# A hybrid RWKV-7 decoder step on one core: engine clocks with measured overheads, steps emitted by VectorE's backlog, and a transposed block made by a transposition

## The chip, the cores and the metric

The kernel runs on one core of a Trainium2 chip. The metric is device microseconds from launch to end, the median of several executions of the compiled program. Five engines work side by side, each through its own queue in order: TensorE (PE, with its weight loads shown as PEld), VectorE (DVE), ScalarE (ACT), GpSimd (POOL) and SyncE (SP), which here only starts transfers.

## The reference

One layer of a decoder for 1024 prompt tokens and 8 sequences of 8 tokens (1088 columns in all), with D_MODEL 1024. Cut to what matters:

```python
h = rms_norm(x) * (1 + sc) + sh
P = h @ w_in                       # 1024 x 4352: RWKV columns, pooling columns, gates
# RWKV-7 branch, 8 heads of 64, after token shift:
sa = einsum(S, -kk_t)
S  = S * w_t + sa * (kk_t * a_t) + v_t * k_t        # one 64x64 state per head and token
y  = einsum(S, r_t)                                  # then group norm, bonus, gate g
# pooling branch: causal means over windows 2, 4, 8, 16 minus the token, a 128x128 map per group
merged = sigmoid(gate_A) * (A @ w_br_rwkv) + sigmoid(gate_B) * (B @ w_br_pool)
x = x + gt * (merged @ w_out)
x = x + gt2 * (square(relu(h2 @ w_ff1)) @ w_ff2)     # h2: a second modulated norm
```

All is float32. The outputs are both y and the new shift, pooling and RWKV states.

## The kernel before, in words

Features lie on the partitions, tokens along the free dimension. A float32 product is made of three products in a rounded format: each weight tile of 128 x 512 is loaded (`wraw`), rounded by ScalarE (`whi`), and its remainder is taken by VectorE or GpSimd (`wlo`); activations are stored likewise in pairs (`hx`). A product then is high x high, high x low, low x high. These products are the tiles `mm` in the profile.

The kernel has two phases. Phase 2, from about 790 us on, holds the output projection and the feed-forward layer. Phase 1, up to there, holds the input projection and the RWKV and pooling branches, and only phase 1 is touched by the change.

In phase 1 the PE's order is written out by a planner, `Pace.run`. It has one background, `stream`, the products of the input projection (34 blocks of 128 output columns, each 72 products, in the order of a list of jobs) followed by those of the pooling output; and four foregrounds, generators that emit small steps between the background's products: `heads` (four pairs of heads, f = 0 to 3, one after another), `chains` (the 16 chunks of 64 tokens of a pair, in sequence), `pools` and `or_rows`. A foreground step yields what it waits for. `Need` is a wait until the step's operands and PSUM banks are forecast to be ready. The forecast comes from `Clocks`, which keeps for every other engine a list of busy stretches, puts each emitted instruction into it at a guessed duration (`place`), and notes when its output will be there. So the planner's time `pace.t` is a guess, and PE itself runs the products in the order that results. If the real operand is later than the guess, PE waits and everything behind it waits too. The order on VectorE, ScalarE and GpSimd is set by the tile framework's own scheduler from the order of emission.

A pair of heads goes through `front` (decay, keys, and their norms, almost all on VectorE over 512 and 576 columns), `scores` with `unit` (64 x 64 score blocks by PE), `inverse` (16 x 16 triangular blocks inverted row by row on VectorE: 15 steps of one product and one reduction), `level` (the 32 x 32 and 64 x 64 blocks joined by PE in small products), `affine`, and then the chain. `bonus` and `post` (group norm and gate of the pair before) run beside `inverse` and `level`; for the last pair `post(3)` runs after its chain. `post(3)` takes its three column pieces one by one: a mean product and a variance product with the block of ones (`kct`), root, reciprocal, affine map, bonus, gate, then the pair `hx` that is the last operand of phase 2's first products.

A job of the background can be held: the job of the second gate block after each pooling group g has `hold = ("op", g)`, so the background gives nothing until `pools` has emitted group g's products (`w<-px,plw`). While it is held, foreground steps alone are emitted.

In `level` the products stand on the 32 x 32 blocks of all chunks: `n16` by `xd` (64 products, `w<-hv,hv`), then the block `nd` by `zd` (64, `w<-iv,hv`) and the transposed one, `zd` by `nd`, for half of the blocks (32, `w<-hv,iv`), which is then copied by VectorE to `x32`; then `ao` by `x32` and `pt` by `z` (32 each). Each of them takes two records in the profile. `inverse` spaces its 15 steps by a fixed time:

```python
            yield 200 + 4 * t * t
```

Of the kernel before, what the change touches and what calls it, by code (L numbers as in the profile page):

```python
# [78 lines left out]
class Clocks:  # L79


    TABLE = {AF.Sqrt: 1, AF.Exp: 2, AF.Tanh: 2}

    def __init__(self, pace):
        self.pace, self.on = pace, False
# [34 lines left out]
    def free(self, key, bufs, k=1):  # L120

        ring = self.slots.get(key, [])
        return max([self.last(ring[j - bufs]) for j in range(k) if len(ring) >= bufs - j] or [0.0])

    def place(self, eng, t, ns):

        b = self.busy[eng]
        k = len(b)
        while k and b[k - 1][0] >= t + ns:
            k -= 1  # L130
        for i in range(max(k - 12, 0), len(b) + 1):
            lo = max(t, b[i - 1][1] if i else 0.0)
            if i == len(b) or b[i][0] >= lo + ns:
                b.insert(i, (lo, lo + ns))
                return lo
        return t

    def op(self, eng, name, a, kw):
        aps = [x for x in list(a) + list(kw.values()) if hasattr(x, "tensor")]
        out, ins = aps[0], aps[1:]  # L140
        n = math.prod(out.shape[1:])
        if "dma" in name:
            t = max([self.pace.t - 4000, self.touch(out, False)] + [self.touch(x, True) for x in ins])
            t += 2000 + out.shape[0] * n * 4 / 220 if out.shape[0] <= P else 4000
        else:
            m = max([n] + [math.prod(x.shape[1:]) for x in ins])
            if eng == "scalar":
                ns = 160 + 0.9 * n
                tb = self.TABLE.get(next((x for x in a[2:3]), None), 0)
                if tb and tb != self.table:  # L150
                    ns, self.table = ns + 1300, tb
            elif eng == "gpsimd":
                ns = 250 + (0.5 if "memset" in name else 2.2) * m
            elif name == "reciprocal":
                ns = 60 + 6.65 * n
            elif name == "transpose":
                ns = 2.05 * n
            elif "scan" in name:
                ns = 150 + 2.1 * n
            elif "reduce" in name:  # L160
                ns = 90 + 1.25 * m
            else:
                ns = 150 + (0.8 if name == "tensor_scalar" else 1.05 if n > 100 else 1.6) * n
            ns += 60
            t = max([self.pace.t - 4000, self.touch(out, False)] + [self.touch(x, True) for x in ins])
            t = self.place(eng, t, ns) + ns + 120
        for x in ins:
            self.note(x, t, True)
        self.note(out, t, False)
# [41 lines left out]
class Need:  # L211
# [4 lines left out]

    def at(self):
        return max([self.k.clocks.ready(*self.aps)] + [self.k.clocks.free(b, self.k.pb[b], self.banks.count(b)) for b in set(self.banks)])

    def __call__(self):  # L220
        return self.at() <= self.k.pace.t
# [82 lines left out]
class K:  # L304
# [37 lines left out]
    def product(self, out, *ins):  # L342
        if self.clocks.on:
            for x in ins:
                self.clocks.note(x, self.pace.t, True)
            self.clocks.note(out, self.pace.t + 180, False)

    def need(self, *aps, banks=("w",), wait=500):
        return Need(self, aps, banks, wait)
# [415 lines left out]
    def front(self, f):  # L765

        nc, io = self.nc, self.io
# [8 lines left out]
        k, kk = self.wt(), self.wt()  # L776
# [31 lines left out]
        for c0, n in FH:  # L808
            s, cs = slice(c0, c0 + n), slice(c0 // 64, (c0 + n) // 64)
            t, a, x = t1[:, s], tha[:, s], k[:, s]  # L810
            nc.vector.tensor_scalar(t, t, 1.0, None, op0=ALU.add)
            nc.vector.tensor_tensor_scan(t, self.kscan[:, :n], t, 0.0, ALU.mult, ALU.add)
            m = min(n, NPR - c0)
            nc.scalar.activation(ev[:, c0 // 64:(c0 + m) // 64, 1:65], cut(t1[:, c0:c0 + m]), AF.Exp, scale=-HC)
            if m < n:
                nc.scalar.activation(es[:, :, 1:9], cut8(t1[:, NPR:NT]), AF.Exp, scale=-HC)
            nc.scalar.activation(t, t, AF.Exp, scale=HC)

            nc.vector.scalar_tensor_tensor(kk[:, s], x, self.par("k_k", f), kk[:, s], op0=ALU.mult, op1=ALU.mult)
            g = bk[:, cs, 0, :]  # L820
            nc.vector.tensor_scalar(g, cut(a), self.hp[:, 8 + f:9 + f], self.hp[:, 12 + f:13 + f], op0=ALU.mult, op1=ALU.add)
            nc.vector.tensor_tensor(cut(x), cut(x), g, op=ALU.mult)
            nc.vector.scalar_tensor_tensor(a, a, 1.0, kk[:, s], op0=ALU.add, op1=ALU.mult)
            for h, hs in enumerate(HB):
                nc.vector.tensor_tensor(bk[hs, cs, h, :], cut(x[hs]), cut(t[hs]), op=ALU.mult)
                nc.vector.scalar_tensor_tensor(bk[hs, cs, 1 - h, :], cut(a[hs]), 0.5, cut(t[hs]), op0=ALU.mult, op1=ALU.mult)
            if c0 == 0:
                self.cur = dict(bk=bk, end=end, kk=kk, r=r, ev=ev, es=es, z=self.z, qs={})
# [3 lines left out]
        yield X(8 + f)  # L832
        nc.vector.scalar_tensor_tensor(k, r, self.par("r_k", f), k, op0=ALU.mult, op1=ALU.mult)
        q = [self.row(self.p1, "wt", 5, F32R) for _ in range(2)]
        self.halves(k, *q)
# [118 lines left out]
    def inverse(self, d):  # L954
# [15 lines left out]
        for t in range(1, 16):  # L970
            pr = prod[:, :2 * t * t].rearrange("p (b j i) -> p b j i", b=2, i=t)
            nc.vector.tensor_tensor(pr, at[:, :, t, 0:t].unsqueeze(2).to_broadcast([P, 2, t, t]),
                                    tt[:, :, 0:t, 0:t].rearrange("p b i j -> p b j i"), op=ALU.mult)
            nc.vector.tensor_reduce(tt[:, :, t, 0:t], pr, axis=AX.X, op=ALU.add)
            yield 200 + 4 * t * t
        ex = self.iv()
        nc.scalar.activation(quad(ex)[:, :, :, 0, :], tt, AF.Copy, scale=half[0])
        nc.vector.tensor_scalar(quad(ex)[:, :, :, 1, :], tt, half[1], None, op0=ALU.mult)
# [11 lines left out]
    def level(self, d):  # L990
# [1126 lines left out]
```

## Time and profile before

| | |
|---|---|
| median of 3 runs | 1656.93 us (1653.83 to 1658.22) |
| the profiled execution's own time | 1658.37 us |
| its span in the profile | 1656.5 us |
| PE busy | 1585.9 us, 96% of the span |
| VectorE busy | 1093.8 us, 66% |
| ScalarE busy | 677.1 us, 41% |
| mean granted TensorE clock | 0.977 |

The profiled execution lasts 1.9 us longer than its span (launch and end) and is 1.4 us above the median of the runs. Rows of the profile name an instruction as output<-inputs by the program's names; for a product the moving operand stands first, the stationary one second. "Idle before" is the time that the engine stood still just before the instruction, with what ended it. The granted clock is the share of full speed that TensorE was given.

### The profile page before, as it was taken

To read this page: it belongs to the slowest core of one execution; us is meant where nothing else is said; L and a number is where in the kernel's file an instruction comes from. 1 tells how busy PE (TensorE), PEld (TensorE's weight loads), DVE (VectorE), ACT (ScalarE), POOL (GpSimd) and SP (SyncE) were. 2 spreads that over 40 slices of the span, in tenths; PEclk is the share of its full clock that TensorE was granted. 3 is DMA by queue.
4 is the path that set the end of the run, shared out by engine and by line. 5 is a ranking of instruction groups with operands and counts; after the bars stand their busy time and mean duration, and the time that the engine had idled before them with its cause. 6 is when DMAs were issued, how large, how long until landed. Compare 5 with 4: busy or idle time off the path is not lost.

```text
span 1656.5 us, 35576 instructions
## 1 busy us (share of the span) xinstructions
PE 1585.9 (96%) x14619; PEld 1485.1 (90%) x14619; DVE 1093.8 (66%) x1916; ACT 677.1 (41%) x1299; POOL 135.4 (8%) x200
## 2 busy tenths in 40 slices
PE   4999999989899889999999999999999999999997
PEld 2899888878788779988989999999999999999997
DVE  5576638583948474746543578999866887666775
ACT  4454344444334453443222455222333443434551
POOL 0110001000100010000430130000000042000000
PEclk9999999997999899999999999999999999999999
DMA  9232513323223313474687446566434997655663
GB/s 346 86 108 87 196 47 111 99 90 112 70 104 129 103 55 114 175 276 147 223 326 238 159 160 223 187 222 228 158 141 146 374 359 263 201 198 164 210 203 121
DMA packets 121859, 288.31 MB, mean 174 GB/s; under 512 B 21120, under 2 KB 26752, under 8 KB 121696
## 3 DMA queue, kind: packets, MB, share of 16 engines
q1 hardware_dynamic: 113312, 264.65, 46.2%
q10 hardware_dynamic: 8240, 20.95, 3.8%
q8 instruction: 115, 1.88, 0.5%
q14 instruction: 48, 0.39, 0.1%
q0 software_dynamic: 144, 0.44, 0.1%
HBM read 208.70 MB, written 77.28 MB: 173 GB/s over the span
## 4 chain that ended last, share of the span: by engine, by line
PE 47%; DMA 3%; DVE 3%; issue 1%; POOL 0%; ACT 0%; SPq 0%; DVEq 0%; ACTq 0%; POOLq 0%
PE mm L340 31%; PE wc L340 10%; PE w L340 5%; DMA hid<-in_w_ff 1%; DVE hx L184 1%; DMA hid<-in_w_ada_mlp 1%; DMA mg<-in_w_ff 1%; DVE wlo L184 0%; DMA t<-d_t 0%; DVE mg L184 0%; DMA d_t<-hx 0%; POOL t L184 0%; DVE t L184 0%; DVE sw L184 0%; PE wc L359 0%
## 5 line engine op out<-in xcount | busy, mean ns | idle before, releaser
L340 PE MATMUL mm<-hx,whi 128*128 128x362 f32 (+2 forms) x2944 | 695.2, 324 | 2.9 <-ACT px L184 1.8
L340 PEld LDWEIGHTS mm<-hx,whi 128*128 128x128 f32 x2944 | 502.3, 192 | 31.7 <-issue 16.3
L340 PE MATMUL mm<-hx,wlo 128*128 128x362 f32 (+2 forms) x1472 | 466.1, 317 | 2.2 <-DVE wlo L184 1.8
L340 PEld LDWEIGHTS mm<-hx,wlo 128*128 128x128 f32 x1472 | 282.1, 192 | 2.8 <-DVE wlo L184 2.1
L340 PE MATMUL mm<-mg,whi 128*128 128x272 f32 (+2 forms) x1312 | 249.6, 289 | 0.1
L340 PEld LDWEIGHTS mm<-mg,whi 128*128 128x128 f32 x1312 | 205.6, 189 | 4.5 <-issue 3.4
L340 PE MATMUL mm<-mg,wlo 128*128 128x272 f32 (+2 forms) x656 | 188.5, 287 | 0.0
L340 PE MATMUL wc<-hx,whi 128*128 128x272 f32 x896 | 170.5, 287 | 0.0
L340 PEld LDWEIGHTS wc<-hx,whi 128*128 128x128 f32 x896 | 140.3, 188 | 0.0
L184 ACT ACTIVATE whi<-hid 128x512 fp32r<-128x512 f32 x128 | 80.4, 630 | 140.5 <-PE mm L340 57.3
L340 PE MATMUL wc<-hx,wlo 128*128 128x272 f32 x448 | 128.9, 288 | 1.1 <-DVE wlo L184 1.1
L340 PEld LDWEIGHTS mm<-mg,wlo 128*128 128x128 f32 x656 | 123.5, 188 | 0.0
L184 DVE TENSOR_TENSOR wlo<-hid,whi 128x512 fp32r<-128x512 f32 x128 | 88.0, 688 | 47.1 <-ACT whi L184 46.4
L184 DVE TENSOR_TENSOR wlo<-wraw,whi 128x512 fp32r<-128x512 f32 x84 | 60.9, 726 | 78.4 <-ACT whi L184 78.2
L184 ACT ACTIVATE whi<-wraw 128x512 fp32r<-128x512 f32 x100 | 62.8, 628 | 104.2 <-PE mm L340 65.2
L340 PE MATMUL w<-hx,whi 128*128 128x272 f32 (+1 forms) x480 | 97.8, 298 | 0.0
L340 PEld LDWEIGHTS wc<-hx,wlo 128*128 128x128 f32 x448 | 84.2, 188 | 1.4 <-DVE wlo L184 1.3
L184 POOL TENSOR_TENSOR hx<-hx,rs 128x64 f32<-128x64 f32 x24 | 38.2, 1592 | 565.1 <-DMA mg<-in_w_ff 376.6
L340 PEld LDWEIGHTS w<-hx,whi 128*128 128x128 f32 x480 | 77.8, 190 | 0.0
L340 PEld LDWEIGHTS mm<-mg,hx 128*128 128x128 f32 x576 | 72.9, 188 | 5.0 <-issue 5.0
L340 PE MATMUL mm<-mg,hx 128*128 128x272 f32 (+2 forms) x576 | 75.5, 290 | 0.0
L184 DVE RECIPROCAL wt<-wt 128x182 f32<-128x182 f32 (+3 forms) x52 | 57.6, 1160 | 22.0 <-ACT wt L184 22.0
(270 smaller groups left out, 2391.9 us busy)
## 6 DMA issues: line engine op xcount, KB each, us to landing
t<-d_t SPq DMA_DIRECT2D x56, 544.0 KB, 5.0
hid<-in_w_ff SPq DMA_DIRECT2D x110, 256.0 KB, 3.9
d_t<-hx SPq DMA_DIRECT2D x102, 272.0 KB, 2.2
hid<-in_w_ff SPq DMA_DIRECT2D x42, 512.0 KB, 3.9
wraw<-in_w_in SPq DMA_DIRECT2D x68, 256.0 KB, 2.9
mg<-in_w_ff SPq DMA_DIRECT2D x58, 256.0 KB, 5.4
hid<-in_w_ada_mlp SPq DMA_DIRECT2D x24, 512.0 KB, 5.2
d_th<-px SPq DMA_DIRECT2D x22, 544.0 KB, 3.0
```

The costliest lines, as they stand in the source:

```text
L184: return f(*a, **kw)
L340: return self.nc.tensor.matmul(out, lhsT, rhs, **kw)
```

## The change

Three things, all in phase 1.

The forecast: an instruction of VectorE now occupies its engine for its duration less 80 ns, one of ScalarE for its duration less 95 ns, one of GpSimd for 60 ns less (before: 60 ns more for each), and its output is forecast 60 ns after the duration (before: 180 ns after it).

The emission: a new wait, `Room`, holds a step until the forecast backlog of VectorE is at most 1000 ns (in `front`, twelve times per pair) or 500 ns (in `inverse`, in place of the fixed spacing).

The level: the 32 transposed products and the two copies go; VectorE transposes the 32 x 32 blocks of the product `ps` straight from PSUM into `x32`, and one PSUM bank less is asked for.

```diff
+    OVER = {"vector": 80, "scalar": 95}
...
+    def backlog(self, eng):
+        return max([b[1] for b in self.busy[eng][-12:]] or [0.0])
...
-            ns += 60
             t = max([self.pace.t - 4000, self.touch(out, False)] + [self.touch(x, True) for x in ins])
-            t = self.place(eng, t, ns) + ns + 120
+            t = self.place(eng, t, ns - self.OVER.get(eng, 60)) + ns + 60
...
+class Room:
+    wait = 0
+    def at(self):
+        return self.k.clocks.backlog(self.eng) - self.ns
+    def __call__(self):
+        return self.at() <= self.k.pace.t
...
+    def room(self, ns=1000, eng="vector"):
+        return Room(self, eng, ns)
...
         for c0, n in FH:
+            yield self.room()
             nc.vector.tensor_scalar(t, t, 1.0, None, op0=ALU.add)
...
-            yield 200 + 4 * t * t
+            yield self.room(500)
...
-        yield self.need(nd, zd, banks=("w", "w"))
-        ps, px = self.ps("w"), self.ps("w")
+        yield self.need(nd, zd)
+        ps = self.ps("w")
...
-        for c in range(16):
-            for g in G[::2]:
-                self.mm(at(px, g, c), zd[g, c, :], nd[g, c, :], **tp(g))
         x32 = cut32(self.hv())
-        for g in G[::2]:
-            nc.vector.tensor_copy(x32[g], cut32(px)[g])
+        nc.vector.transpose(x32, cut32(ps))
```

Three places show how the order moves. The first is on PE, pair f = 1, where the background is held on pooling group 1 (`px` and `plw`: that group's products; `bones` with `wt`: sums of `post(0)`; `sw`: its gate; `iv`, `hv`, `ao`, `z`: `level`). Before, these rows stand in one piece, with no background product among them:

```order
L340 MATMUL w_4015<-px_3665,plw_3396 128x364
L340 MATMUL w_4019<-wt_3696,bones 128x364
L340 MATMUL w_4019<-wt_3697,bones 128x364
L340 MATMUL w_4027<-wt_3696,bones 128x362
L340 MATMUL w_4027<-wt_3697,bones 128x362
L340 MATMUL w_4035<-wt_3696,bones 128x362
L340 MATMUL w_4035<-wt_3697,bones 128x362
L340 MATMUL w_4049<-px_3665,plw_3396 128x362
L340 MATMUL w_4053<-wt_4046,sw_4043 128x364
L340 MATMUL w_4056<-iv_3796,hv_3979 32x32 x64
L340 MATMUL w_4057<-hv_3979,iv_3796 32x32 x32
L340 MATMUL w_4161<-hv_4154,ao_3009 32x32 x32
```

Now the group's first two pieces stand among background products (`mm`), 45 of them after the group's own columns are done:

```order
L358 MATMUL mm_3860<-hx_213,whi_3830 128x362
L358 MATMUL mm_3860<-hx_214,whi_3830 128x362
L358 MATMUL mm_3860<-hx_213,wlo_3831 128x362
L358 MATMUL w_3924<-px_3729,plw_3394 128x364
L358 MATMUL w_3928<-px_3729,plw_3394 128x362
L358 MATMUL mm_3858<-hx_215,whi_3830 128x364
L358 MATMUL mm_3858<-hx_216,whi_3830 128x364
```

The third piece and the level's first products follow 18 products later, the level's next 12 later, and the sums of `post(0)` stand far ahead, before the inverse. No background product waits for the hold any more.

The second place is VectorE around the level of pair f = 0 (`iv`, `hv`: the inverse's blocks; `d`, `ds`: token shift of the projection; `am`: a modulation row). Before:

```order
L184 STREAM_TRANSPOSE hv_1890<-iv_1886 128x16x32
L184 STREAM_TRANSPOSE iv_1889<-iv_1886 128x16x32 x2
L184 TENSOR_TENSOR wlo_1936<-wraw_1933,whi_1935 128x512
L184 SCALAR_TENSOR_TENSOR d_1945<-px_1807,part,d_1945 128x1024
L184 SCALAR_TENSOR_TENSOR ds_1946<-px_1807,part,d_1945 128x64
L184 TENSOR_TENSOR hv_2046<-w_1981,kct 128x512
L184 COPY hv_2163<-w_2066 32x512 x2
L184 TENSOR_TENSOR am<-wc_2170,part 128x72
```

After:

```order
L187 STREAM_TRANSPOSE hv_1871<-iv_1867 128x16x32
L187 STREAM_TRANSPOSE iv_1870<-iv_1867 128x16x32 x2
L187 TENSOR_TENSOR wlo_1894<-wraw_1891,whi_1893 128x512
L187 TENSOR_TENSOR hv_1974<-w_1909,kct 128x512
L187 STREAM_TRANSPOSE hv_2049<-w_1984 128x512
L187 TENSOR_TENSOR wlo_2164<-wraw_2161,whi_2163 128x512
```

The two copies have become one transposition, which reads the product itself.

The third place is PE at the end of phase 1 (`w<-wt,kct`: mean and variance products of `post(3)`; `mm` with `hx` and `whi`: first the pooling output, then phase 2's first products). Before, the last variance product stands here, and 69 background products follow it before phase 2 begins:

```order
L340 MATMUL mm_8616<-hx_7708,wlo_8543 128x364
L340 MATMUL w_8622<-wt_8415,kct 128x362
L340 MATMUL mm_8617<-hx_7708,whi_8542 128x362
L340 MATMUL mm_8617<-hx_7710,whi_8542 128x362
L340 MATMUL mm_8617<-hx_7708,wlo_8543 128x362
```

Now the variance product of the middle piece and the mean product of the last one come nine products before the end, and the last variance product is phase 1's last row:

```order
L358 MATMUL w_8542<-wt_8438,kct 128x362
L358 MATMUL w_8551<-wt_7329,kct 128x362
L358 MATMUL mm_8508<-hx_7513,whi_8305 128x364
L358 MATMUL mm_8508<-hx_7515,whi_8305 128x364
L358 MATMUL mm_8508<-hx_7513,wlo_8306 128x364
L358 MATMUL mm_8509<-hx_7513,whi_8305 128x362
L358 MATMUL mm_8509<-hx_7515,whi_8305 128x362
L358 MATMUL mm_8509<-hx_7513,wlo_8306 128x362
L358 MATMUL mm_8510<-hx_7513,whi_8305 128x362
L358 MATMUL mm_8510<-hx_7515,whi_8305 128x362
L358 MATMUL mm_8510<-hx_7513,wlo_8306 128x362
L358 MATMUL w_8568<-wt_8438,kct 128x362
```

Phase 2's first products (`mm_8626`) follow it at once. The last pair's `level` begins 135 background products later in the order than before (2559 ahead of it instead of 2424), those of pairs 1 and 2 begin 15 and 132 later, that of pair 0 begins 39 earlier.

More of the change, by code (lines that the diff above doesn't have):

```diff
@@ L218, in at, with __init__ @@
         return max([self.k.clocks.ready(*self.aps)] + [self.k.clocks.free(b, self.k.pb[b], self.banks.count(b)) for b in set(self.banks)])
+    def __call__(self):
+        return self.at() <= self.k.pace.t
+class Room:
+    wait = 0
+    def __init__(self, k, eng, ns):
+        self.k, self.eng, self.ns = k, eng, ns
+    def at(self):
+        return self.k.clocks.backlog(self.eng) - self.ns
     def __call__(self):
@@ L817, in front @@
             nc.scalar.activation(t, t, AF.Exp, scale=HC)
+            yield self.room()
             nc.vector.scalar_tensor_tensor(kk[:, s], x, self.par("k_k", f), kk[:, s], op0=ALU.mult, op1=ALU.mult)
@@ L821, in front @@
             nc.vector.tensor_scalar(g, cut(a), self.hp[:, 8 + f:9 + f], self.hp[:, 12 + f:13 + f], op0=ALU.mult, op1=ALU.add)
+            yield self.room()
             nc.vector.tensor_tensor(cut(x), cut(x), g, op=ALU.mult)
@@ L824, in front @@
             for h, hs in enumerate(HB):
+                yield self.room()
                 nc.vector.tensor_tensor(bk[hs, cs, h, :], cut(x[hs]), cut(t[hs]), op=ALU.mult)
@@ L827, in front @@
             if c0 == 0:
+                yield self.room()
                 self.cur = dict(bk=bk, end=end, kk=kk, r=r, ev=ev, es=es, z=self.z, qs={})
@@ L832, in front @@
         yield X(8 + f)
+        yield self.room()
         nc.vector.scalar_tensor_tensor(k, r, self.par("r_k", f), k, op0=ALU.mult, op1=ALU.mult)
```

## The prediction

> **What bounds the kernel now.** First the page: how busy each engine is, and the granted clock over the span.
>
> ```profile
> span 1656.5 us, 35576 instructions
> PE 1585.9 (96%) x14619; PEld 1485.1 (90%) x14619; DVE 1093.8 (66%) x1916; ACT 677.1 (41%) x1299; POOL 135.4 (8%) x200
> PEclk9999999997999899999999999999999999999999
> ```
>
> PE is the bound and no other engine is near. So the time is PE's work, its waits, and what a low clock costs; the reader should see that the clock dips only in the first half. Second, stretches of the span (us, busy time of PE, PEld, DVE, ACT, POOL with instructions, granted clock, DMA): phase 1, phase 2, and four places in phase 1.
>
> ```profile
> 60.00:790.00 730.00, 694.97 (x7736) 620.70 (x7736) 453.90 (x817) 318.93 (x646) 44.12 (x116) 0.95 0.35 119
> 790.00:1656.50 866.50, 854.40 (x6691) 839.62 (x6689) 603.44 (x1047) 329.50 (x614) 88.43 (x69) 1.00 0.62 215
> 361.40:392.40 31.00, 23.76 (x361) 17.47 (x360) 15.92 (x18) 16.73 (x27) 0.00 (x0) 0.56 0.24 81
> 196.00:210.00 14.00, 12.16 (x293) 11.40 (x291) 3.56 (x6) 6.06 (x10) 0.00 (x0) 0.76 0.25 85
> 528.00:548.00 20.00, 16.66 (x439) 15.43 (x437) 8.13 (x13) 8.54 (x17) 1.42 (x5) 0.83 0.29 90
> 697.00:717.00 20.00, 17.26 (x382) 16.28 (x382) 12.51 (x14) 13.28 (x19) 1.26 (x1) 0.83 1.02 402
> ```
>
> Phase 2 has full clock; the change doesn't touch it. In phase 1 PE stands still for 730 - 695 = 35 us, and a clock of 0.95 costs about 5% of 730 = 36 us: some 71 us could be had. Third, what ended PE's waits in phase 1 (us in total, times, longest):
>
> ```profile
> PE w L340 <- issue: 10.2, 5, 3.3
> PE w L340 <- ACT wt L184: 8.9, 6, 2.6
> PE w L340 <- DVE px L184: 4.8, 2, 4.0
> PE wc L340 <- DVE S L184: 4.0, 4, 1.4
> ```
>
> "issue" means that no other engine was waited for.
>
> **The held stretch.** The timeline of PE, first warm background products, then the stretch of pair 1 in which the background is held on pooling group 1:
>
> ```profile
> 679.77 0.50 PE L340 MATMUL mm<-hx,whi 128*128 128x362 f32 x2
> 680.28 0.49 PE L340 MATMUL mm<-hx,whi 128*128 128x362 f32 x2
> ...
> 364.74 1.46 PE L340 MATMUL w<-wt,bones 128*128 128x362 f32 x4 [2.20 <-ACT wt L184]
> 369.62 1.55 PE L340 MATMUL w<-wt,sw 128*128 128x364 f32 x2 [1.80 <-issue]
> 390.71 0.81 PE L340 MATMUL mm<-hx,whi 128*128 128x362 f32 x2
> ```
>
> Three warm products start every 0.50 us, so 0.165 us each; the same pair of products at 390.71 lasts 0.81 instead of 0.49. In 361.4 to 392.4 PE is busy 23.76 us at a clock of 0.56: 13.3 us of full-speed work in 31.0, so 17.7 us are lost. The order after has group 1's products 45 background products (7.4 us) behind the group's last column and ahead of the hold, and the level's products 12 to 15 background products apart, so the same 13.3 us of work stands among warm products. What could remain is a plain wait for the group's VectorE work. The nearest rows are two such waits for other groups and group 1's own work:
>
> ```profile
> 307.11 0.85 PE L340 MATMUL w<-px,plw 128*128 128x364 f32 x2 [0.84 <-DVE px L184]
> 456.00 1.80 PE L340 MATMUL w<-px,plw 128*128 128x364 f32 x4 [3.95 <-DVE px L184]
> ...
> 351.49 1.25 DVE L184 TENSOR_TENSOR d<-px 128x1038 f32<-128x1038 f32 x1
> 357.04 0.16 DVE L184 COPY px<-zf 128x3 f32<-128x3 f32 x1
> ```
>
> From 351.49 to 357.20 is 5.7 us, inside the 7.4, but other VectorE work can slip between. I keep back their mean, 2.4 us, rounded up: **-15 us**, ends -18 and -12 (17.7 less 3.95, and the 1.7 us that a half-clock window adds).
>
> **The transposed products.** PE's timeline at the level of pairs 0, 2, 3, and the group's sum:
>
> ```profile
> 199.03 0.89 PE L340 MATMUL w<-hv,iv 32*32 32x32 f32 x45
> 201.76 0.74 PE L340 MATMUL w<-hv,iv 32*32 32x32 f32 x18 [1.84 <-issue]
> ...
> 539.84 0.74 PE L340 MATMUL w<-hv,iv 32*32 32x32 f32 x19 [3.34 <-issue]
> ...
> 709.76 0.42 PE L340 MATMUL w<-iv,hv 32*32 32x32 f32 x13 [2.37 <-issue]
> ...
> L340 PE MATMUL w<-hv,iv 32*32 32x32 f32 x256 | 7.4, 221 | 6.0 <-issue 6.0
> ```
>
> At full clock 45 records take 0.89 us, so 256 take 5.1; the 7.4 holds half-clock ones, which I count in the next term. **-5 us**, ends -7.4 and -4: products on either side keep their own cost.
>
> VectorE's side, groups of phase 1:
>
> ```profile
> L184 DVE STREAM_TRANSPOSE hv<-iv 128x512 f32<-128x512 f32 x4 | 4.8, 1207 | 0.7 <-ACT iv L184 0.6
> L184 DVE COPY hv<-w 32x512 f32<-32x512 f32 x8 | 5.5, 684 | 13.4 <-PE w L340 13.3
> ```
>
> Out go eight copies (5.5 us), in come four transpositions from PSUM. No row shows that source; from SBUF it is 1.21 us, nearest in size and kind, and twice that is my upper end, 2.4. The product that reads `x32` stands 15 background products (2.5 us) behind `ps`, so 1.21 hides; at 2.4 it would cost up to about 0.5 a pair. I take 0, ends 0 and +2. The bank asked for less can only let the step go earlier: 0.
>
> **The stops at the level.** In pairs 0, 2, 3 PE stops 1.84 + 3.34 + 2.37 = 7.55 us right in or ahead of the transposed products, with nothing to wait for on any engine, and the clock falls behind each: 14 x 0.24 + 20 x 0.17 + 20 x 0.17 = 10.2 us. The burst is 128 records of one product and 64 of the next within 2 us; I read it as PE running out of instructions that are already fetched. The change makes the burst a third shorter. In two of three cases the stop lies in the part that goes; in the third, 13 records before the end of what stays. A stop of that kind can move to the next short products. I take half, **-9 us**, ends -18 and 0.
>
> On the clock, the Trainium skill ("TensorE: Matmul & The Clock Gate", Part 1) says that TensorE falls to half speed after at least one idle window of about 3.4 us. Here half speed also follows a stop of 1.84 us, with a clock of 0.76 over 14 us, so the trace does not agree on the length. By that rule these stops, all under 3.4 us, would not cool PE and this term would be half of 7.55, -4 us, the whole then -20; I follow the rows.
>
> **Forecast and emission elsewhere.** What is left of phase 1's loss is 71 - 17.7 - 17.8 = 36 us, spread over some 20 waits. `Room` keeps `front` and `inverse` from filling VectorE's queue ahead of weight remainders, pooling and reciprocals, which takes away lateness such as 3.95 us at 456.00. Against it, every forecast comes 120 ns sooner (60 behind the duration instead of 180), and PE is in order: where VectorE is late, everything stands. By reading the orders, group 2's products after the change stand 42 background products behind its columns (72 before), with `front`'s steps between its VectorE work, so a wait of about the same size remains there. **0 us**, ends -16 (not quite half of what is left) and +29 (below).
>
> **The end of phase 1.** Around the last variance product of `post(3)`, PE, DVE and ACT:
>
> ```profile
> 784.13 0.77 PE L340 MATMUL w<-wt,kct 128*128 128x362 f32 x2
> ...
> 786.03 2.41 DVE L184 RECIPROCAL wt<-wt 128x182 f32<-128x182 f32 x2
> 791.84 0.53 DVE L184 TENSOR_TENSOR wt<-wt,wt 128x362 f32<-128x362 f32 x1
> ...
> 786.14 0.51 ACT L184 ACTIVATE hx<-wt 128x362 fp32r<-128x362 f32 x1 [0.64 <-DVE wt L184]
> ```
>
> From this product to the last gate multiplication's end are 8.2 us; with the high part (0.51) and a remainder of about that length some 9.2 us till the operand is whole. Before, 69 products (11.4 us) cover it, and 27 of phase 2's that don't need it. After, only those 27 and 6 more stand between: 0.8 + 33 x 0.165 = 6.2 us. So 3 us are uncovered, and VectorE's order there has the middle piece's reciprocal and three updates (2.4 + 3 x 0.5 us) in the same stretch, half of which I count as late: **+4 us**, ends 0 and +8 (all of it late, and one window of half clock).
>
> **The sum:** -15 - 5 - 9 + 0 + 4 = -25 us on the profiled execution (1656.5 span, 1.9 around it, 1658.4), so 1633.4; the median of the runs is 1.4 below that execution: **1632 us**, 1.5% faster. Under 0.3% (5 us) this kernel's measurement can't be told from no change.
>
> **The rivals.**
>
> *More goes than I count.* All stops at the level end (-18 instead of -9) and the other waits give 16: -15 - 5 - 18 - 16 + 4 = -50, 1607 us. For it: VectorE is only 62% busy in phase 1 (453.90 of 730), so lateness is a matter of order, which is what changes. Against: the S waits (4.0 us in four) are a chain's latency, which no order shortens.
>
> *Only the held stretch and the products.* The stops move to the next short products and keep their size: -12 - 5 + 0 + 0 + 4 = -13, 1644 us. For it: the third stop lies in products that stay.
>
> *The change doesn't do what it says:* the waits come back in other places because VectorE's real order is the scheduler's, not that of emission: 1657 us within 5. For it: the pooling wait of group 2 by the orders. Against: the held stretch can't come back, no background product is behind a hold.
>
> *Slower: the forecasts lose their slack.* The place is every PE step that waits for an operand, by the code some 60 a pair, 240 in all. If each comes 0.12 us too early, PE stands 29 us more: -25 + 29 = +4, and with cooling 1663 us. It decides once the mean new wait is over 0.10 us. For it: the chain's S rows show PE already waiting at some steps. Against: before, with 180 ns of slack, those listed waits were of 1 to 4 us each, lateness in queues and not in tenths, and VectorE's durations in the rows above (0.684 for a copy, 2.41 for two reciprocals) are close to what the planner's formulas assume (0.69 and 2.54).
>
> If the stall at the end of phase 1 comes in one piece, the Trainium skill's rule on the clock gate (the same part) would add one cold window of 3.4 us, at half speed 1.7 us; it is inside that term's end.
>
> **How the numbers follow.** My sum: 0.50, own range 1622 to 1642. More: 0.12. Only stretch and products: 0.17. No change: 0.08. Slower: 0.13. The range for 8 in 10 leaves out the lower half of "more" (0.06) and most of "slower" (0.12): 1611 to 1659. Faster by over 0.3%: 0.50 + 0.12 + 0.17 = 0.79; within: 0.08; slower: 0.13.
>
> **What the profile after would show.** The stretch of pair 1: no run of foreground products without `mm` near pooling group 1, and PEclk 9 in that slice instead of 7. `w<-hv,iv` gone, four transpositions `hv<-w` of 1.0 to 2.4 us. "issue" waits of PE in phase 1 near 4 us instead of 10.2. At the border of the phases a wait of the first `mm` with the last `hx`, by VectorE or ScalarE, of 3 to 5 us. Phase 2 as long as before, 866 us within 3. I am wrong if PE's idle time in phase 1 stays near 35 us with many small waits for DVE, or if the border costs over 10 us.

## The result and the profile after

The changed kernel is slower: 1680.8 us (median of 4 runs, 1675.5 to 1684.8) against 1656.4 us for the kernel before (4 runs of the same session, 1653.8 to 1658.2), a ratio of 1.0146 with a 95% interval of 1.0112 to 1.0181. The profiled execution took 1675.5 us, so 17.1 us more than that of before by their spans; it is the fastest of its four runs, and the medians are 24.4 us apart, so the account below covers 17.1 of them. One execution of e1_level, further down, took 8510 us and is left out of its ratio. First the page of after, the lines that answer to those of before:

```profile
span 1673.6 us, 35049 instructions
PE 1579.6 (94%) x14363; PEld 1478.1 (88%) x14363; DVE 1089.8 (65%) x1912; ACT 671.4 (40%) x1295; POOL 138.3 (8%) x200
PEclk9999999999999999989999999999999999999999
```

The granted clock no longer dips in the first half as it did (one slice of 8 is left, at 711 to 753 us), and PE is busy 6.3 us less, yet the span is longer: what was won in work was lost in standing still. Phase 1 in stretches (us, busy time of PE, PEld, DVE, ACT, POOL, granted clock, DMA), first after, then before; the first row of after is the window of the held stretch:

```profile
361.40:392.40 31.00, 29.42 (x412) 28.01 (x410) 14.54 (x23) 11.85 (x22) 1.76 (x3) 1.00 0.59 194
...
200.00:340.00 140.00, 126.58 (x1292) 110.94 (x1286) 93.07 (x179) 59.87 (x131) 12.72 (x30) 0.99 0.26 85
340.00:480.00 140.00, 131.50 (x1435) 116.97 (x1435) 76.78 (x126) 54.80 (x108) 7.04 (x9) 0.95 0.30 96
620.00:720.00 100.00, 87.09 (x794) 76.24 (x794) 72.12 (x139) 45.33 (x101) 7.80 (x8) 0.92 0.47 170
720.00:820.00 100.00, 95.04 (x1237) 84.14 (x1236) 46.45 (x87) 26.51 (x50) 6.96 (x7) 0.97 0.44 155
```

```profile
200.00:340.00 140.00, 136.21 (x1466) 122.79 (x1467) 85.43 (x168) 62.40 (x135) 6.76 (x21) 0.98 0.26 85
340.00:480.00 140.00, 126.82 (x1512) 108.11 (x1513) 89.29 (x146) 57.88 (x115) 8.36 (x16) 0.89 0.29 94
620.00:720.00 100.00, 97.15 (x1083) 91.00 (x1083) 63.43 (x123) 45.17 (x96) 3.54 (x7) 0.95 0.49 176
720.00:820.00 100.00, 98.98 (x1041) 89.49 (x1040) 54.16 (x97) 30.14 (x54) 16.48 (x10) 1.00 0.56 192
```

In 340 to 480 us PE gained 4.7 us of busy time and a better clock. In 200 to 340 it lost 9.6, in 620 to 720 10.1, in 720 to 820 3.9. What ended PE's waits in phase 1 of after (us in total, times, longest):

```profile
PE w L358 <- DMA wt<-d_x: 14.1, 3, 9.0
PE wc L358 <- DVE S L187: 7.1, 6, 2.3
PE w L358 <- issue: 7.0, 4, 2.7
PE w L358 <- DVE tt L187: 4.6, 1, 4.6
PE w L358 <- DVE wt L187: 4.3, 4, 2.5
PE w L358 <- DVE px L187: 3.9, 2, 3.6
```

The first line is the gate of `post(0)` to `post(2)`, which waits for the load of `sg`. Of its three waits (2.52, 2.57 and 9.00 us) only the third is new. In before the loads for the first two gates were issued at 365.93 and 551.52 us and took 3.6 and 3.5 us, and the gates' products began within 0.1 us of the landings, at 369.62 and 555.13, after idle times of 1.80 and 2.49 us that the profile puts down to "issue" and to ScalarE. The new wait in PE's timeline, then the issue of that load in SyncE's queue, then (690 to 722 us) what the DMA engines carried and the load's median time from issue to landing:

```profile
717.29 1.58 PE L358 MATMUL w<-wt,sw 128*128 128x364 f32 x2 [9.00 <-DMA wt<-d_x]
...
707.18 0.32 SPq L187 DMA_DIRECT2D wt<-d_x  x1
```

```profile
DMA packets 3197, 11.45 MB, mean 358 GB/s; under 512 B 368, under 2 KB 368, under 8 KB 3194
...
wt<-d_x SPq DMA_DIRECT2D x1, 544.0 KB, 10.1
```

The load left at 707.18, 1.1 us before PE stood still at 708.29, into DMA engines that carried 358 GB/s in the mean, and took 10.1 us. The same three views of before:

```profile
718.00 0.77 PE L340 MATMUL w<-wt,sw 128*128 128x364 f32 x2
...
707.21 0.32 SPq L184 DMA_DIRECT2D wt<-d_x  x1
...
DMA packets 2896, 10.39 MB, mean 325 GB/s; under 512 B 317, under 2 KB 317, under 8 KB 2891
...
wt<-d_x SPq DMA_DIRECT2D x1, 544.0 KB, 10.2
```

So the load was as slow before, at the same time; but its gate's product stood 10.8 us behind the issue, with other products between, and PE didn't wait. In after a half-clock window of 10.2 us began inside the stop, at 711.39, and PE worked in 4.3 us of it. The stretch around it, with a clock of 0.74 over 20 us:

```profile
704.00:724.00 20.00, 10.78 (x46) 9.16 (x45) 14.14 (x16) 9.55 (x16) 3.01 (x5) 0.74 0.79 310
```

The planner reckons about 0.5 us from the load's emission (it starts such a load 4 us back in time and gives it 4.5), in before and after alike: the change doesn't touch the forecast of loads.

To count all of it: PE's idle time (gaps over 0.2 us between its records) from the first `wlo` product to the last variance product of `post(3)` is 36.2 us before and 51.7 after, behind that 4.8 and 10.8, ahead of it 21.4 and 23.0. The rest of PE's time, from record to record, fell from 1586.7 to 1580.7. Together: 15.5 + 6.0 + 1.6 - 6.0 = 17.1 us.

### The profile page after: what moved, and what is told of

It reads as the page before. It is cut to its first block, busy times and chain, and to the rows that moved or that the text cites. A ratio compares the mean times of both kernels' runs of the same rounds, so it can differ in the third digit from the quotient of the medians.

```text
span 1673.6 us, 35049 instructions
## 1 busy us (share of the span) xinstructions
PE 1579.6 (94%) x14363; PEld 1478.1 (88%) x14363; DVE 1089.8 (65%) x1912; ACT 671.4 (40%) x1295; POOL 138.3 (8%) x200
## 4 chain that ended last, share of the span: by engine, by line
PE 64%; DVE 6%; DMA 5%; issue 1%; ACT 1%; POOL 0%; SPq 0%; DVEq 0%; POOLq 0%; ACTq 0%
PE mm L358 41%; PE wc L358 11%; PE w L358 10%; DMA hid<-in_w_ff 1%; DVE hx L187 1%; DVE wlo L187 1%; DMA wt<-d_x 1%; DVE wt L187 1%; DMA hid<-in_w_ada_mlp 1%; DMA mg<-in_w_ff 1%; DMA t<-d_th 1%; DVE hv L187 0%; DMA wraw<-in_w_br 0%; DVE mg L187 0%; DVE px L187 0%
## 5 line engine op out<-in xcount | busy, mean ns | idle before, releaser
L187 ACT ACTIVATE px<-mm 128x362 f32<-128x362 f32 (+3 forms) x113 | 47.1, 436 | 80.4 <-PE mm L358 76.8
```

Of the source, the lines that this page charges most:

```text
L187: return f(*a, **kw)
```

## The experiments

Theory A: forecasts that come sooner put steps ahead of their operands, and PE stands. Theory B: `Room` shifts the foreground to where its cover is missing. Theory C: the transposition itself costs. From the fifth experiment on also theory D: the time is an accident of each order, without a sign. All ratios are to the kernel before, with 95% intervals.

**The three parts, each alone, and all without Room.** e1_level is the kernel before with the level's hunk of the diff, e2_forecast with `OVER` and the two lines of the forecast, e3_room with `Room` in `front` and `inverse`; e4_no_room is the changed kernel with the waits for `Room` taken out:

```diff
-            yield self.room()        # twelve per pair, in front
...
-            yield self.room(500)
+            yield 200 + 4 * t * t
```

> The kernel before with the level's transposition alone; forecasts and emission are the old ones. Both theories: the 256 short records go, so 4 to 6 us less work; half of the stops at the level (7.6 us and 10 us of low clock before) go or move. Time 1638 to 1652, ratio 0.989 to 0.997. Theory C (the transposition itself costs): it reads PSUM, takes over 2 us each, and the ratio is 1.00 or more.

> The kernel before with the new forecasts alone (no Room, no transposition). Theory A (forecasts that come sooner put steps ahead of their operands): more and longer waits of PE in phase 1, idle time well over 35 us, 1670 to 1690 us. Theory B (Room is what costs, by shifting post's gate and the last pair): this one has no Room, the last chain ends 261 background products earlier than before, so PE's idle time stays near 35 us and the time at 1645 to 1660.

> The kernel before with Room alone in front and inverse (old forecasts, old level). By the order the last pair's level is emitted only when the background has run out. Theory B: the last pair's level, chain and post stand bare at the end of phase 1, some 40 to 80 us of PE mostly waiting, 1690 to 1740 us. Theory A: the old forecasts have their slack, so waits elsewhere stay few; the time is 1650 to 1670, the end costing under 15 us.

> The changed kernel without Room (new forecasts and transposition, inverse's old fixed spacing). Theory A: as slow as the changed kernel or slower, 1675 to 1690 us. Theory B: 1640 to 1655, since the gate and the last pair come early again.

Measured: transposition 0.9973 (0.9958 to 0.9988), forecasts 1.0100 (1.0076 to 1.0124), Room 1.0413 (1.0388 to 1.0438), all without Room 1.0181 (1.0160 to 1.0202). So C falls (the transposition takes 0.7 us in the trace of e1_level, not over 2), A is supported, and so is B: Room alone costs most. Room alone delays the foreground until the background runs out: the last pair's level stands behind all 2736 background products of phase 1 (behind 2424 of them before, 2559 in the changed kernel), and the end of phase 1 is bare. Stretch of e3_room:

```profile
740.00:860.00 120.00, 86.82 (x1297) 66.07 (x1296) 73.49 (x144) 42.40 (x91) 2.39 (x6) 0.70 0.19 66
```

33 of 120 us idle and a clock of 0.70, where before PE was busy 48.98 of 50 us in 740 to 790. The parts don't add up (0.9973, 1.0100 and 1.0413 against 1.0146): the new forecasts bring the chain forward, Room holds it back, and together they leave its end covered.

In e1_level one wait deserves a look, since its label misleads:

```profile
442.08 1.55 PE L340 MATMUL w<-px,plw 128*128 128x364 f32 x2 [15.17 <-issue]
...
441.81 0.16 DVE L184 COPY px<-zf 128x7 f32<-128x7 f32 x1
```

"issue" says that nothing visible was waited for; but the copy that completes the pooling product's operand `px` ends at 441.97, 0.1 us before the product begins, and VectorE's queue ran without a pause from 419 us to that copy. So even the kernel that came out fastest lost 15 us in one backlog of VectorE.

**The halves of the forecast, the opposite sign, and the gate mended.** e5_distances takes only the shorter hold of the engine, e6_ends only the earlier end, e7_later an end 120 ns later than before; e8_gate is the changed kernel with a later landing of `sg`:

```diff
+            t = self.place(eng, t, ns - 60 - self.OVER.get(eng, 60)) + ns + 120   # e5
...
+            t = self.place(eng, t, ns) + ns            # e6 (before: + 120)
...
+            t = self.place(eng, t, ns) + ns + 240      # e7
...
+            if not last:                               # e8, behind the load of sg
+                self.clocks.note(sg, self.pace.t + 11000, False)
```

> The kernel before with one half of the new forecasts alone: each VectorE and ScalarE instruction holds its engine for its duration less 80 or 95 ns (before: plus 60), while an operand still counts as whole 180 ns behind the duration. Theory A (steps of PE come ahead of their operands; the forecast's error adds up along an engine's queue): 140 ns per queued instruction, so this half carries most of the loss of the two halves together (1.0100), 1.006 to 1.009, with 5 to 10 us more of PE waiting for DVE and ACT in phase 1 or behind it. Theory D (the order before fits its waits by adjustment, and any shift of the foreground costs about the same, whichever way it goes): slower too, by any amount up to 1.015, and then the third kernel of this call is slower as well. If the small distances are simply right, as VectorE's rows of before say (a 128x512 tensor_tensor starts the next one 0.59 us later; the new forecast says 0.61, the old 0.75): 1.000 or below.

> The kernel before with the other half alone: an operand counts as whole 60 ns behind the instruction's duration (before: 180), the engine's occupation as before. Theory A: each step of PE that needs an operand comes up to 120 ns sooner, once and not added up: 1.002 to 1.005. The rival of the prediction (240 steps x 0.12 us) gives its full price here: +29 us, 1.017. Theory D: anywhere from 1.00 to 1.015.

> The kernel before with the opposite sign: an operand counts as whole 300 ns behind the duration (before: 180). Theory A: fewer and shorter waits of PE for DVE and ACT in phase 1, 5 to 10 us less idle time; but the foreground comes later (the last pair's level at background product 2634 instead of 2424) and its end finds no background, which costs some 5 us as in the kernel with Room alone: together 0.995 to 1.002. Theory D: slower, 1.005 to 1.015, with waits of another kind in place of the old ones.

> The changed kernel with one forecast mended: the gate's operand sg in post counts as landed 11 us behind the emission of its load instead of 0.5 us (pairs 0 to 2), so that the gate's product stands some 66 background products further on. If the three waits for this load (2.5 + 2.6 + 9.0 us) and the half-clock stretch behind the last (10.2 us at half speed, 5 us lost) are a loss of their own: 14 to 19 us less than the changed kernel, a ratio to before of 1.003 to 1.006. If that time is only a symptom of the foreground's place and goes to the next wait: 1.012 to 1.015 as the changed kernel.

Measured: e5 1.0046 (1.0029 to 1.0063), e6 1.0015 (1.0002 to 1.0028), e7 1.0000 (0.9985 to 1.0015), e8 1.0173 (1.0145 to 1.0201). The prediction's rival of 240 steps at 0.12 us each had its full test in e6 and is out: 1.0015 instead of 1.017, with 9.5 us more idle time in phase 1 instead of 29. e8 is the most telling miss: the three waits for the load are gone, and the time is not better. What ended PE's waits in phase 1 of e8_gate:

```profile
PE w L358 <- issue: 15.5, 5, 12.0
PE wc L358 <- DVE S L187: 8.3, 6, 2.7
PE mm L358 <- DVE px L187: 6.1, 2, 5.3
PE w L358 <- DVE px L187: 5.4, 2, 3.6
```

In place of 9.0 us for the load there is a wait of 12.0 ahead of a pooling product, as in e1_level: its "issue" ends 0.1 us after VectorE's last copy into `px` (454.78 + 0.17, the product at 455.05). On this run the 14.1 us were where the time was lost rather than why; but e8 is a new order too, with an accident of its own (below), so one run can't settle it.

**Room and transposition without the new forecasts; slack given back; a change that means nothing.** e9_room_level is the changed kernel with the old forecast lines. e10_slack is e4_no_room, e11_after_slack the changed kernel, each with a later end; e12_ten_ns is the kernel before with 10 ns more:

```diff
-            t = self.place(eng, t, ns - self.OVER.get(eng, 60)) + ns + 60
+            t = self.place(eng, t, ns - self.OVER.get(eng, 60)) + ns + 300        # e10; e11: + 180
...
-            t = self.place(eng, t, ns) + ns + 120
+            t = self.place(eng, t, ns) + ns + 130                                 # e12
```

> The changed kernel with the old forecasts put back: Room and the transposition alone. If the new forecasts cost the same 1% wherever they stand, this runs at 1.003 to 1.008. If what Room costs is the place of the foreground (Theory B: each step waits till VectorE's planned backlog is below 1 us, and with old forecasts that backlog is longer), the last pair's level has no background products behind it any more (all 2736 of phase 1 are ahead of it; 2559 in the changed kernel) and the chain of pair 3 stands bare on PE: 1.03 to 1.04, as Room alone (1.0413) less the transposition's gain.

> New forecasts and transposition without Room (the kernel that ran at 1.0181), with one number changed: an operand counts as whole 300 ns behind its instruction's duration instead of 60. Nothing else moves but what follows from it. Theory A (a step that is forecast too early makes PE stand): the waits of PE in phase 1 fall from 56 us to 40 or less and the ratio to 0.998 to 1.008. Theory D (the time is an accident of each order, the forecasts' size has no sign): no drift towards 1.00, anything from 1.005 to 1.025 with about as much waiting, 50 to 60 us.

> The changed kernel with one number changed: an operand counts as whole 180 ns behind its instruction's duration (as before) instead of 60; engine occupation, Room and transposition stay. Theory A: the waits fall by some 10 us and the ratio from 1.0146 to 1.005 to 1.010. But Room and slack both delay the foreground (last pair's level at product 2655 of 2736, 2559 in the changed kernel), so Theory B has the end of phase 1 bare: some 10 us more waiting behind 790 us, and 1.015 to 1.025.

> The kernel before with a change that means nothing: an operand counts as whole 190 instead of 180 ns behind the duration. It moves steps by a few products. Theory A: the same time, 0.998 to 1.002. Theory D: any change of the order moves the time by some tenths of a per cent, so 0.995 to 1.008, and outside 0.998 to 1.002 as likely as not.

Measured: e9 1.0311 (1.0290 to 1.0333), e10 0.9996 (0.9984 to 1.0008), e11 1.0104 (1.0083 to 1.0124), e12 1.0064 (1.0040 to 1.0088). e9 confirms B: Room needs the early forecasts. From e4 to e10 one number, 60 to 300 ns, takes the ratio from 1.0181 to 0.9996 and the idle time of phase 1 from 56.2 to 44.6 us, as A says, though not to the 40 us that A had named. But 10 ns, which mean nothing, cost the kernel before 0.64%, as D says. So single ratios of this size can't be read as the worth of an edit.

**Neighbours.** e13_after70 and e14_after50 are the changed kernel with 70 and 50 ns, e15_slack290 is e10 with 290, e16_level_later joins e1 and e7, e17_before110 is the kernel before with 10 ns less, e18_level130 is e1 with 10 ns more: in each, one number of the forecast's last term.

> The changed kernel with 70 instead of 60 ns behind the duration, a change that means nothing by itself. Theory A (lost slack): the loss belongs to small forecasts, so 1.009 to 1.020 as the changed kernel (1.0146). Theory D (each order its own accident, a spread of about 0.6%): anywhere from 0.998 to 1.02.

> The changed kernel with 50 instead of 60 ns. Theory A: 1.009 to 1.022. Theory D: anywhere from 0.998 to 1.02. If this and the run with 70 ns lie on both sides of 1.009, the spread of orders is as large as the loss itself.

> New forecasts and transposition without Room, with 290 instead of 300 ns behind the duration (300: 0.9996; 60: 1.0181). Theory A: 0.995 to 1.008, far from 1.0181, with 40 to 50 us of waits in phase 1. Theory D: the gain from 60 to 300 ns was luck of one order, and this one may lie anywhere up to 1.018.

> The kernel before with the transposition and the old forecasts set later (300 ns behind the duration, engine held 60 ns longer): the two parts that did not lose, together. Theory A: the transposition's 0.27% and nothing from the forecasts, 0.994 to 1.000. Theory D: that, with its own accident on top, 0.992 to 1.006.

> The kernel before with 170 instead of 180 ns behind the duration, a change that means nothing; by the order only few steps move, by 3 products at most for a pair's level. Theory A (the forecasts' size decides): 0.998 to 1.003. Theory D (the order struck decides, and the kernel before is a lucky one): 1.002 to 1.010, as its neighbour with 190 ns (1.0064).

> The kernel with the transposition alone (0.9973) with 190 instead of 180 ns behind the duration. Theory A: 0.995 to 1.000, the transposition's gain holds. Theory D: 0.997 to 1.008; above 1.002 it says that the gain of 0.27% was the order's and not the transposition's.

Measured: e13 1.0095 (1.0074 to 1.0117), e14 1.0036 (1.0016 to 1.0055), e15 1.0056 (1.0035 to 1.0077), e16 1.0111 (1.0090 to 1.0132), e17 1.0077 (1.0050 to 1.0105), e18 1.0007 (0.9994 to 1.0020). The changed kernel is the slowest of its row (50, 60 and 70 ns), the kernel before the fastest of its own (170, 180 and 190 ns); e13 and e14 lie on both sides of 1.009, which e14's expectation had named as the sign that the scatter of orders is as large as the loss. Neither theory's ranges hold alone: those of A miss e5, e12, e14, e16 and e17 (and e6, e11 and e18 narrowly), those of D miss e7, e10 and e16. What 10 ns do, by PE's waits in phase 1 of e17_before110 and then of before:

```profile
PE w L340 <- issue: 13.8, 7, 3.4
PE wc L340 <- DVE S L184: 12.4, 6, 3.4
```

```profile
PE w L340 <- issue: 10.2, 5, 3.3
PE wc L340 <- DVE S L184: 4.0, 4, 1.4
```

The chain's waits for `S` went from 4.0 to 12.4 us. Two of them, 2.56 and 2.28 us, lie at 260 to 266 us, where PE's clock has a dip (8 in the seventh slice) that before doesn't have:

```profile
PEclk9999998997999799999999999999999999999999
```

The transposition's 0.27% doesn't survive this test: 0.9973, 1.0007 and 1.0111 have a mean of 1.0030, as have the five kernels with the old level and the old engine times (1, 1.0064, 1.0077, 1.0000, 1.0015: 1.0031). e1_level as it stands came out 0.27% faster than before, but no edit is shown to be the reason.

**A and D together.** The planner counts waits of its own: the leaps of `pace.t` at a product whose operand it forecasts later, and while the background is held. They are reckoned while the program is written and are no time of the chip, but they say how careful an order is. Beside them the idle time of PE in phase 1 on the chip, up to the last variance product of `post(3)`, and the ratio, for all but the two orders that run out of background (e3, e9):

```
             waits planned, us   idle on the chip, us   ratio
after              19                 51.7             1.0146
e8_gate            19                 57.0             1.0173
e13_after70        21                 51.2             1.0095
e14_after50        33                 48.3             1.0036
e5_distances       52                 51.8             1.0046
e11_after_slack    53                 52.9             1.0104
e2_forecast        56                 45.7             1.0100
e4_no_room         65                 56.2             1.0181
e15_slack290       83                 48.9             1.0056
e10_slack          86                 44.6             0.9996
e6_ends            92                 45.7             1.0015
e18_level130      103                 45.2             1.0007
e17_before110     114                 43.8             1.0077
e1_level          114                 44.7             0.9973
before            120                 36.2             1
e12_ten_ns        125                 43.3             1.0064
e16_level_later   139                 49.5             1.0111
e7_later          147                 36.2             1.0000
```

The eight orders above the gap at 70 us stand idle 51.9 us in the mean and have a mean ratio of 1.0110; the ten below, 43.8 us and 1.0030. (That variance product comes at 723 us in e4 and at 817 in e8; with the idle time behind it the means are 60.6 and 50.0 us.) The difference of 0.80% has a standard error of 0.24%, from the scatter inside the groups (0.54 and 0.44%). Sorted by their edits instead, the six with both new forecast lines (after, e2, e4, e8, e13, e14) have a mean of 1.0122 and the five with both old ones to within 10 ns (before, e1, e12, e17, e18) 1.0024, a difference of 0.98% with a standard error of 0.30%. So early forecasts go with about 0.8 to 1% in the mean, and each order adds an accident of about half a per cent. The split at 70 us was chosen with the numbers in view, and the kernels are variants of each other, so this is an estimate.

## Why the prediction was wrong

Predicted were -25 us, measured are +17.1 by the spans of the two profiles. By its steps:

**The held stretch, -15: right.** The window 361.4 to 392.4 has PE busy 29.42 us at a clock of 1.00, where it was 23.76 at 0.56. Group 1's products wait 0.29 us, where 2.4 were kept back. The three other groups wait 3.60, 2.72 and 4.57 us instead of 0.84, 3.95 and 1.23: together 4.9 us more, which no term held. Two of them in PE's timeline:

```profile
317.16 1.16 PE L358 MATMUL w<-px,plw 128*128 128x364 f32 x3 [3.60 <-DVE px L187]
...
516.24 2.19 PE L358 MATMUL w<-px,plw 128*128 128x364 f32 x4 [4.57 <-DVE tt L187]
```

**The transposed products, -5: right, and the transposition was cheaper than its range.** The group of after beside the one from SBUF:

```profile
L187 DVE STREAM_TRANSPOSE hv<-w 128x512 f32<-128x512 f32 x4 | 2.9, 717 | 12.4 <-PE w L358 12.4
L187 DVE STREAM_TRANSPOSE hv<-iv 128x512 f32<-128x512 f32 x4 | 4.5, 1130 | 0.3 <-ACT iv L187 0.3
```

0.72 us each, where 1.21 was taken and 2.4 was the end; 2.9 us of VectorE in place of 5.5. The row from SBUF was no close relative: its block is read in pieces of 16 elements and written in strides, the product in one run of 512.

**The stops at the level, -9: about right.** Three stops remain, each shorter: 4.3 us at `w<-iv,hv` instead of 7.55 at the two kinds, and a half-clock window behind one of them only, so 3.2 us of standing still are gone, and some 8.5 of the 10.2 by the clock:

```profile
L358 PE MATMUL w<-iv,hv 32*32 32x32 f32 x512 | 5.7, 193 | 4.3 <-issue 4.3
```

The prediction read these stops as PE running out of fetched instructions, and the traces bear that out. The DMA queue q8 brings packets of 16 KiB of kind "instruction", one for every 254 or so records of PE and PEld:

```profile
q8 instruction: 113, 1.85, 0.4%
```

The traces of this case hold 43 stops of over 0.9 us inside or right ahead of 32x32 products that are labelled "issue", and at each of them PE resumes 1.2 to 1.6 us after such a packet has landed. No run moves the packets alone.

On the clock, the Trainium skill ("TensorE: Matmul & The Clock Gate", Part 1) asks for an idle window of about 3.4 us ahead of half speed. After the stop of 1.47 us at 742.70 a half-clock window of 3.41 us began at 745.52; none began behind those of 1.56 and 1.29 us. So the trace does not agree on the length, as before the change.

**The end of phase 1, +4: about right.** Two waits at the border, 1.20 and 2.15 us, make 3.35. The second is the one that was forecast, for the last `hx`; the first, ended by VectorE's `px`, was not. (The step's own working, 3 us and half of 3.9, gives 5 and not 4.)

```profile
807.63 0.60 PE L358 MATMUL mm<-hx,whi 128*128 128x362 f32 x2 [1.20 <-DVE px L187]
...
814.53 1.00 PE L358 MATMUL mm<-hx,whi 128*128 128x362 f32 x2 [2.15 <-ACT hx L187]
```

**Forecast and emission elsewhere, 0: this step failed.** Outside the held stretch (7.2 us idle) and the level's stops (7.55) PE was idle 21.4 us in phase 1 before; after, outside the stops, 47.4: +26 us, near the upper end of +29. The new waits brought new half-clock windows: by the prediction's steps, what half speed costs while PE works should have fallen from 30.8 us ahead of phase 2 to some 15, and it fell to 20.5. Phase 2 with its border took 6.7 us more instead of 4 (a load of `hid` was waited for 1.7 us longer), and the start, whose code is unchanged, had 1.6 us more idle time.

The count of the whole says the same. The prediction's terms make -8.3 us of idle time in phase 1, +4 behind it and -20.6 in PE's records; measured were +15.5, +6.0 and -6.0, and +1.6 ahead of phase 1. Of the 42 us between forecast and result, about 24 are idle time in phase 1, 5.5 half speed, 3.5 the start and the border, and 9, in PE's records, have no place of their own. The sign that the prediction had named, idle time that stays near 35 us, came in a stronger form: it rose to 51.7, and more in waits of 3 to 9 us than in many small ones.

Two errors stand behind the 0. First, the slack: the prediction counted 120 ns once a step and weighed it against small waits, and the rows it read ("lateness in queues and not in tenths") were right that lateness comes in lumps. But they were taken as a reason against a loss, where they are its form: less slack doesn't make every wait longer by 0.1 us, it sends some steps of PE past the point where a whole queue of VectorE, or a load, is still ahead of its operand. The forecast of distances itself is good (a 128x512 product on VectorE starts the next one 0.60 us later by the trace; 0.61 new, 0.75 old), and yet the kernel with it alone, e5, stands idle 15.6 us longer in phase 1 and came out 0.46% slower, which is no more than any new order may cost. That the old error was slack for all that the planner doesn't know, such as a load that lands after 10.1 us, is a reading of these rows; no run tests it by itself. The rival with this name had the right direction, a chance of 0.13, and the wrong price: its own test, e6, gave 0.15%.

Second, the order struck: the prediction took the kernel before as a neutral start, from which a term can be worth 0. Its two neighbours at 10 ns stand 0.64 and 0.77% above it. Any new order was to be expected some 5 us slower (the mean of 1.0031 over the five of its family, itself among them) with a scatter of about 8 us, and no term held that. Of the 1.46%, by these means, about 0.3% is what leaving that order costs, 0.8% the early forecasts, and the rest the accident of this one order; whether Room costs anything once the forecasts are early stays open (with it 1.0146, 1.0095 and 1.0036, without it 1.0181).

## What to carry to other kernels

An order tuned by trial is one draw that was kept: before an edit to a planner is priced, run the planner with a constant moved by next to nothing, and take the scatter (here half a per cent) and the mean of those neighbours as the base. On an engine that runs in order a step placed too early stops everything behind it, while a step placed too late costs only cover, as long as there is cover left (e3 and e9 ran out of it). So a forecast that is right in the mean may still be too early, and slack in a planner is to be kept, or replaced by forecasts of what it stood for (a queue's backlog, a busy DMA). Where a wait is mended and the time stays, as in e8, the wait may have been the place of the loss and not its cause. And the label of a wait is a guess: "issue" stood here for a load, for VectorE's queue and for an instruction packet.

## What the runs showed of the hardware

A transposition of 128x512 in blocks of 32x32 on VectorE took 0.72 us from PSUM, where it reads and writes one run of 512 elements, and 1.13 from SBUF, where it reads pieces of 16 and writes in strides (the rows above); which of the two differences counts is not shown. PE's stops in bursts of 32x32 products end 1.2 to 1.6 us after an instruction packet of 16 KiB has landed, in all 43 of them. The load of `sg`, 544 KB, landed 3.5 and 3.6 us after its issue at the first two gates of before and 10.2 us after it at the third, where the DMA engines carried 325 GB/s in the mean (10.1 in after, at 358). Two loads of the same size in e1_level's quiet stretch (415 to 445 us, 70 GB/s):

```profile
DMA packets 2186, 2.11 MB, mean 70 GB/s; under 512 B 1161, under 2 KB 1673, under 8 KB 2185
...
wt<-d_x SPq DMA_DIRECT2D x2, 544.0 KB, 4.0
```
